# Holding all TensorE instructions in written order through the attention of a two-layer streaming encoder

## The chip, the cores and the metric

The kernel runs on one core of a Trainium2 chip. The metric is device time in microseconds, the median of 3 runs. Five engines work side by side, each through its own instructions in a fixed order: TensorE (PE; its weight loads are PEld), VectorE (DVE), ScalarE (ACT), GpSimd (POOL) and SyncE (SP), which here issues nearly all DMAs. Waits between engines go by semaphores.

## The reference

Input `x` is (1, 2048, 1024) float32. Layer 0 is a gated pooling mixer, layer 1 strictly causal stick-breaking attention with 16 heads of 64 channels; each ends with a gated embedding add. Cut to what matters:

```python
# layer 0
h = rms_norm(x, a_norm);  u, z = split(h @ a_w_in)
pooled = trailing_means(u, windows 2, 4, 8, 16 by channel group) - u
x = x + ((pooled @ w_group) * scale * silu(z)) @ a_w_out
x = x + (p[0] @ ple_w[0]) * sigmoid(x @ ple_gate_w[0])
# shared keys and values, layer 1
k, v = split(rms_norm(x, kv_norm) @ w_kv);  k = rms_norm(heads(k), k_norm)
q, z = split(rms_norm(x, b_norm) @ b_w_in); q = rms_norm(heads(q), b_q_norm)
beta = sigmoid(q . k / 8)
A[t, s] = beta[t, s] * prod over s < j < t of (1 - beta[t, j])     # s < t
x = x + ((A @ v) * silu(z)) @ b_w_out
x = x + (p[1] @ ple_w[1]) * sigmoid(x @ ple_gate_w[1])
```

## The kernel before

**Tiling.** The 2048 frames are four chunks of 512. Activations lie channel-major: 128 channels by 512 frames in a tile. Every matrix product is made of three float32r matmuls per 128 rows of the contraction, high by high, high by low, low by high, where "low part" is what float32r rounding left over (`split`, `put_split`, and L754 for the attention weights).

**Two streams of work.** `stream()` (a generator) yields after each projection matmul: per chunk `first_part` (mixer, output projection, gate, then z, q, k, v of the first eight heads), `second_part` (q, k, v of the other eight), and after all chunks `post` (output projection and gate of layer 1). The projections' weights come in units of 512 KB through nine `wpair` buffers: raw loads (`wraw`) that are split on the spot, or ready pairs that an earlier pass stored (`once`, `wf`). `keep` prepares the 36 units of layer 1's last weights beforehand and stores them; it loads `kraw` and stores `kp`.

The attention is a loop over 160 slots (chunk of queries, head, chunk of keys) of four steps each, 640 steps. One step n does: `turn`, four transposes (L748) of running products into a `psa` bank, copied by ScalarE (L751) with the low part taken by DVE (L754); `front`, two score matmuls (L728, L729) into a `psl` bank, a sigmoid (L731) and, one step later, the running product on DVE (L736, TENSOR_TENSOR_SCAN); and `gather`, two matmuls (L761, L762) into `pso`. The transposes of a slot lag its score products by 5 steps, the gathers by 7 (`LAG_T`, `LAG_G`). In between, `fill` advances the projection stream by a share given by `rate`: about 27 projection matmuls a step in the first chunk, 13 in the second, 7 in the third and fourth. Each of the PSUM tags `psd` (projections), `psl`, `psa` (also for `pst`, small transposes and sums) and `pso` has two banks.

**What sets the order.** The code is written in one order, but the framework schedules: it simulates a timeline by its own costs and issues what it takes to be ready, so instructions of one engine can change places. `tc.keep_in_program_order` ties an instruction behind the one written before it on its engine. Before the change this holds for the running products (L736), the low parts (L754), and one projection matmul in six of `product` when the third or fourth chunk is in the attention (`state["pin"]`, L225).

**Keys and queries** are stored two heads to a tile (`qd`, `kd`: 128 rows, high and low side by side). A key tile is then loaded by two DMAs of 64 partitions, a query pair (`qa` high over low, `qb` low over high) by four.

Of the kernel before, what the change touches and what calls it, by code (L numbers as in the profile page):

```python
# [36 lines left out]
def trunk_kernel(ctx, tc, x, p, a_norm, wu_t, wz_a, w_group, a_scale, a_w_out, kv_norm, w_kv,  # L37
                 k_norm, b_norm, b_w_q, b_w_z, b_q_norm, b_w_out, ple_a, ple_b, gate_a, gate_b, out):
    nc = tc.nc
    V, A, G, T = nc.vector, nc.scalar, nc.gpsimd, nc.tensor  # L40

    cp = ctx.enter_context(tc.tile_pool(name="cp", bufs=1))
    dram = ctx.enter_context(tc.tile_pool(name="dram", bufs=1, space=bass.MemoryType.DRAM))
# [31 lines left out]
    qd = [[scratch(f"qd{s}_{m}", [P, 2, W5]) for m in range(NH // 2)] for s in range(NSUB)]  # L75
    kd = [[scratch(f"kd{s}_{m}", [P, 2, W5]) for m in range(NH // 2)] for s in range(NSUB)]
    vd = [[scratch(f"vd{s}_{b}", [8, P, 4, P]) for b in range(2)] for s in range(NSUB)]
    ve = [[scratch(f"ve{s}_{b}", [4, W5]) for b in range(2)] for s in range(NSUB)]

# [18 lines left out]
    state = {"solo": True, "pin": False, "turn": 0, "lo": 0}  # L98

    def bank(tag, nm):  # L100
        return psum.tile([P, W5], F32, tag=tag, name=nm)
# [117 lines left out]
    def product(ps, us, acts, c0, back):  # L219
        n = len(acts)  # L220
        i = 0
        for u, kts in us:
            for e, kt in enumerate(kts):
                hi, lo = (u[:, l, e, c0 : c0 + P] for l in range(2))
                ins = T.matmul(ps, hi, acts[kt][:, 0], start=(i == 0), stop=False)  # L225
                if state["pin"] and e == 0:
                    tc.keep_in_program_order(ins)
                yield
                T.matmul(ps, hi, acts[kt][:, 1], start=False, stop=False)  # L229
                yield  # L230
# [256 lines left out]
    def kvq(s, kind, b):  # L487
        ck = chunk[s]
        us = take(KT)
        for j in range(4):  # L490
            tk = slice(j * P, (j + 1) * P)
            ps = dense()
            for kt in range(KT):
                u = us[kt][0]
                for xh, wh in ((0, 0), (1, 0), (0, 1)):
                    T.matmul(ps, ck["x2"][kt][:, xh, tk], u[:, wh, 0], start=(kt == 0 and xh == wh),  # L496
                             stop=(kt == KT - 1 and wh == 1))
                    if j == 3 and wh:
                        give_back()
                    yield  # L500
                if j == 0 and kt == 5 and "r2" not in ck:
                    ck["r2"] = token_norm(ck["acc2"], "y")
                if lag and (j, kt) in ((1, 2), (1, 5), (2, 1), (2, 4)):
                    lag.pop(0)()
            rj = ck["r2"][:, j : j + 1]
            settle()
            (valued if kind == "v" else keyed)(s, kind, b, j, ps, rj)
# [25 lines left out]
    def keyed(s, kind, b, j, ps, rj):  # L533
        qs = row("qs")
        q8 = qs.rearrange("q (h d) -> q h d", d=HD)
        A.activation(out=qs, in_=ps, func=AF.Identity, scale=rj)
        sq = tmp("sqq")
        A.activation(out=sq, in_=qs, func=AF.Square)
        ss = pool.tile([P, 8], F32, tag="ssq", name="ssq")
        V.tensor_reduce(out=ss, in_=sq.rearrange("q (h d) -> q h d", d=HD), op=ALU.add, axis=AX.X)  # L540
        rq = pool.tile([P, 8], F32, tag="rq", name="rq")
        rsqrt_mean(rq, ss, HD, "q")
        V.tensor_tensor(out=q8, in0=q8, in1=rq.unsqueeze(2).to_broadcast([P, 8, HD]), op=ALU.mult)
        rows = chunk[s].setdefault((kind, b), [])
        rows.append(qs)
        if j < 3:
            return

        def finish(m):
            pt = turned()  # L550
            for i in range(4):
                T.transpose(pt[:, i, :], rows[i][:, m * P : (m + 1) * P], ident)
            pt = pt.rearrange("q j t -> q (j t)")
            hl = t4("hl")
            if kind == "k":
                split(hl, pt, V)
            else:
                A.activation(out=hl[:, 0], in_=pt, func=AF.Identity, scale=gqk)
                V.scalar_tensor_tensor(out=hl[:, 1], in0=pt, scalar=gqk, in1=f(hl[:, 0]),
                                       op0=ALU.mult, op1=ALU.subtract)  # L560
            nc.sync.dma_start(out=(kd if kind == "k" else qd)[s][4 * b + m], in_=f(hl))

        for m in range(4):
            lag.append(lambda m=m: finish(m))
# [22 lines left out]
    def gate_z(s):  # L587
# [20 lines left out]
        for b in range(1 if first else 0, 4):  # L608
            us = take(4)
            for k in range(2):  # L610
                o = 2 * b + k
                ps = dense()
                for i, _ in enumerate(product(ps, us, ck["x2"], k * P, k)):
                    if first and o == 2 and i == 9:
                        ck["rb2"] = bcast(ck["r2"], "y")
                    if first and o in (2, 3) and i == 21:
                        zr = first[o - 2]
                        V.tensor_tensor(out=zr, in0=zr, in1=ck["rb2"], op=ALU.mult)
                        put(o - 2, zr)
# [72 lines left out]

    def load_q(c, h):
        qa, qb = qryt("qa"), qryt("qb")
        rows = qd[c][h // 2][h % 2 * HD : (h % 2 + 1) * HD]
        for l in range(2):
            nc.sync.dma_start(out=f(qa)[l * HD : (l + 1) * HD], in_=rows[:, l])
            nc.sync.dma_start(out=f(qb)[(1 - l) * HD : (2 - l) * HD], in_=rows[:, l])
        return qa, qb

    def load_k(kc, h):
        kk = keyt("kk")
        rows = kd[kc][h // 2][h % 2 * HD : (h % 2 + 1) * HD]
        for l in range(2):
            nc.sync.dma_start(out=f(kk)[l * HD : (l + 1) * HD], in_=rows[:, l])
        return kk

    def load_v(kc, h):
# [118 lines left out]
        pass  # L827

    until((0, 0))
    state["solo"] = False  # L830
    begin(0)
    begin_v(0)
    for _ in range(24):
        next(run)
    owed = 0.0
    count = 0
# [1 line left out]
    def fill(share):  # L838
        nonlocal owed, count
        owed += share  # L840
        while owed >= 1.0:
            next(run, None)
            owed -= 1.0
            count += 1
            if count % 36 == 0 and kept:
                keep(*kept.pop(0))

    scan = None
    for n in range(4 * len(slots) + LAG_G):
# [3 lines left out]
        low = turn(active[i2], j2) if 0 <= i2 < len(slots) else None  # L853
        due, scan = scan, None
        if i < len(slots):
            state["pin"] = slots[i][0] >= NSUB - 2
            if j == 0 and i + 1 < len(slots):
                begin(i + 1)
            if j == 3 and i + 1 < len(slots):
# [82 lines left out]
```

## Time and profile before

| | us |
|---|---|
| median of 3 runs | 2831.26 (2830.03 to 2836.04) |
| the profiled execution, own time | 2833.48 |
| its span, first to last instruction | 2831.7 |
| busy: PE / DVE / ACT / POOL | 2729.6 / 1832.6 / 1275.0 / 873.3 |
| granted TensorE clock, mean | 0.986 |
| DMA moved | 643 MB, 227 GB/s in the mean |

A span is the time from the first to the last profiled instruction. Busy time is the union of an engine's instructions; PE's are pipelined, so they overlap. "Idle before" counts the time in which an engine did nothing just before an instruction, and the releaser is what ended that wait. Windows are in us from the start of the span. The projections alone run up to about 385 us, when the first score product starts (385.1); the last starts at 2729.3; then the fourth chunk's `post` runs alone.

### The profile page before, as it was taken

The numbers are of one execution on the slowest core, as the hardware profiler recorded it, in microseconds if no ns is written. First come the engines' busy times: TensorE is split into PE (matmuls) and PEld (weight loads), VectorE is DVE, ScalarE is ACT, GpSimd is POOL, SyncE is SP. The second block draws the span as 40 slices with busy tenths as digits, with TensorE's granted clock in tenths as the row PEclk, the third lists the DMA queues.
The fourth block names the chain that finished last, engine by engine and source line by source line (L and its number), as shares of the span: only waits on it lengthen the run. The fifth ranks groups of instructions, "written<-read, shape, count | busy, mean of one in ns | idle before, by whom it ended". The sixth has DMA issues, their size and how long they took to land.

```text
span 2831.7 us, 38727 instructions
## 1 busy us (share of the span) xinstructions
PE 2729.6 (96%) x13400; PEld 2250.0 (79%) x13400; DVE 1832.6 (65%) x2369; ACT 1275.0 (45%) x2496; POOL 873.3 (31%) x699
## 2 busy tenths in 40 slices
PE   7999989989999999999999999989999999999999
PEld 7888867867888888888877887868877888887767
DVE  5645446747344776655568978657667777767772
ACT  4435543445344345444444555444444444444441
POOL 1354533546533244442322434211221101111002
PEclk8999999999999999999999999999999999999999
DMA  5647899979887845668775454676586768666535
GB/s 212 223 142 277 318 340 355 325 218 302 293 289 278 255 142 174 196 226 272 254 242 163 142 158 152 225 262 206 159 276 192 249 207 263 208 194 225 169 121 185
DMA packets 300496, 643.43 MB, mean 227 GB/s; under 512 B 51206, under 2 KB 83974, under 8 KB 300300
## 3 DMA queue, kind: packets, MB, share of 16 engines
q1 hardware_dynamic: 298716, 639.63, 68.6%
q8 instruction: 106, 1.74, 0.2%
q10 hardware_dynamic: 1584, 1.33, 0.2%
q14 instruction: 90, 0.74, 0.1%
HBM read 471.43 MB, written 161.02 MB: 223 GB/s over the span
## 4 chain that ended last, share of the span: by engine, by line
PE 78%; DMA 8%; DVE 7%; ACT 2%; issue 2%; POOL 1%; SPq 1%; ACTq 0%; DVEq 0%; POOLq 0%
PE psd L496 15%; PE psd L225 11%; PE psd L229 11%; PE psd L232 11%; PE psa L748 7%; PE pso L762 4%; PE psl L729 4%; PE psl L728 3%; PE pso L761 3%; DVE pp L736 3%; PE psd L251 2%; PE psd L248 2%; PE psd L246 2%; DMA wpair<-once 2%; DVE at L754 1%
## 5 line engine op out<-in xcount | busy, mean ns | idle before, releaser
L736 DVE TENSOR_TENSOR_SCAN pp<-pp,floor 128x512 f32<-128x512 f32 (+3 forms) x640 | 779.0, 1219 | 5.2 <-ACT pp L731 4.6
L496 PE MATMUL psd<-wpair,x 128*128 128x512 f32 x2304 | 582.9, 395 | 10.0 <-ACT wpair L137 3.9
L754 DVE TENSOR_TENSOR at<-psa,at 128x512 fp32r<-128x512 f32 (+3 forms) x640 | 378.7, 595 | 312.9 <-ACT at L751 311.1
L496 PEld LDWEIGHTS psd<-wpair,x 128*128 128x128 f32 x2304 | 425.4, 189 | 98.6 <-ACT wpair L137 5.8
L751 ACT CAST at<-psa 128x512 fp32r<-128x512 f32 (+3 forms) x640 | 330.9, 523 | 378.3 <-PE psa L748 358.7
L731 ACT ACTIVATE pp<-psl 128x512 f32<-128x512 f32 (+3 forms) x640 | 333.4, 535 | 305.8 <-PE psl L729 194.8
L748 PE MATMUL psa<-ident,pp 128*128 128x128 f32 x2176 | 357.4, 276 | 45.0 <-DVE at L754 23.7
L748 PEld LDWEIGHTS psa<-ident,pp 128*128 128x128 f32 x2176 | 272.9, 141 | 132.0 <-DVE at L754 38.7
L762 PE MATMUL pso<-at,vv 128*128 128x512 f32 (+3 forms) x640 | 275.1, 430 | 0.6 <-DVE at L754 0.6
L728 PE MATMUL psl<-kk,qa 128*128 128x512 f32 (+3 forms) x640 | 244.3, 382 | 13.2 <-DMA kk<-kd 9.8
L761 PE MATMUL pso<-at,vv 128*128 128x512 f32 (+3 forms) x640 | 238.7, 374 | 7.6 <-DMA once<-kp 5.4
L729 PE MATMUL psl<-kk,qb 128*128 128x512 f32 (+3 forms) x640 | 236.0, 370 | 0.0
L225 PE MATMUL psd<-x,wpair 128*128 128x512 f32 x592 | 233.5, 394 | 0.0
L232 PE MATMUL psd<-x,wpair 128*128 128x512 f32 x592 | 232.5, 393 | 0.0
L229 PE MATMUL psd<-x,wpair 128*128 128x512 f32 x592 | 232.5, 393 | 0.0
L225 PE MATMUL psd<-xp,wpair 128*128 128x512 f32 x512 | 203.5, 398 | 0.5 <-DMA wpair<-once 0.5
L229 PE MATMUL psd<-xp,wpair 128*128 128x512 f32 x512 | 201.7, 394 | 0.0
L232 PE MATMUL psd<-xp,wpair 128*128 128x512 f32 x512 | 201.2, 394 | 0.0
L133 POOL TENSOR_TENSOR wpair<-wraw,wpair 128x512 fp32r<-128x512 f32 x98 | 139.0, 1423 | 153.6 <-ACT wpair L131 152.5
L728 PEld LDWEIGHTS psl<-kk,qa 128*128 128x128 f32 x640 | 122.8, 192 | 40.8 <-ACT pp L731 11.2
L465 POOL TENSOR_TENSOR xj<-x 128x512 f32<-128x512 f32 x64 | 106.9, 1675 | 139.6 <-DVE sg L476 131.9
L761 PEld LDWEIGHTS pso<-at,vv 128*128 128x128 f32 x640 | 122.0, 191 | 27.7 <-ACT at L751 11.0
(162 smaller groups left out, 4621.0 us busy)
## 6 DMA issues: line engine op xcount, KB each, us to landing
wpair<-once SPq DMA_DIRECT2D x384, 512.0 KB
once<-wpair SPq DMA_DIRECT2D x80, 512.0 KB
kk<-kd SPq DMA_DIRECT2D x320, 128.0 KB
vv<-vd SPq DMA_DIRECT2D x160, 256.0 KB
wpair<-wf SPq DMA_DIRECT2D x48, 512.0 KB
once<-kp SPq DMA_DIRECT2D x36, 512.0 KB
wraw<-in_a_w_out_dram SPq DMA_DIRECT2D x64, 256.0 KB
wraw<-in_gate_a_dram SPq DMA_DIRECT2D x64, 256.0 KB
```

The costliest lines, as they stand in the source:

```text
L225: ins = T.matmul(ps, hi, acts[kt][:, 0], start=(i == 0), stop=False)
L229: T.matmul(ps, hi, acts[kt][:, 1], start=False, stop=False)
L232: T.matmul(ps, lo, acts[kt][:, 0], start=False, stop=(i == n))
L496: T.matmul(ps, ck["x2"][kt][:, xh, tk], u[:, wh, 0], start=(kt == 0 and xh == wh), stop=(kt == KT - 1 and wh == 1))
L728: T.matmul(ps[:, :w], qa[:, qs], kk[:, :w], start=True, stop=False)
L729: T.matmul(ps[:, :w], qb[:, qs], kk[:, :w], start=False, stop=True)
L731: A.activation(out=pp[:, r0:], in_=ps[:, :w], func=AF.Sigmoid, scale=-1.0)
L736: V.tensor_tensor_scan(out=pp[:, r0:][:, ::-1], data0=pp[:, r0:][:, ::-1], data1=least, initial=1.0 if st["diag"] else st["carry"][j], op0 ...
L748: T.transpose(pt[:, j * P : (j + 1) * P], pp[:, r0 + kt * P : r0 + (kt + 1) * P], ident)
L754: V.tensor_tensor(out=at[:, 1, cs], in0=pt[:, cs], in1=f(at[:, 0, cs]), op=ALU.subtract))
L761: T.matmul(po[:, cs], vv[:, kt, :], at[:, 0, cs], start=(st["diag"] and kt == 0), stop=False)
L762: T.matmul(po[:, cs], vv[:, kt, :], at[:, 1, cs], start=False, stop=(st["last"] and kt == 3))
```

## The change

It does five things.

1. `nc.tensor` is wrapped by a class `T` whose `matmul` and `transpose` call `tc.keep_in_program_order` on every instruction as long as `state["hold"]` is set: from the first attention slot to the last. The partial pin in `product` goes. All of PE's instructions are then recorded at the wrapper's two lines (L46 matmuls, L50 transposes).
2. Three places are moved later in the written order: the sums of squares for `r2` from the sixth to the end of the eight contraction blocks in `kvq`; the broadcast of `r2` in `gate_z` from the 10th to the 21st matmul; and `keep` starts only once chunk 1's first half of heads is done.
3. Before the first step, 60 projection matmuls are written instead of 24.
4. `qd` and `kd` hold one head each, high rows over low rows, so a key tile is one DMA of 128 partitions, a query pair three DMAs instead of four; what was one store is two of 64 partitions.
5. The running products and the low parts were tied already and stay so.

```diff
-    V, A, G, T = nc.vector, nc.scalar, nc.gpsimd, nc.tensor
+    V, A, G = nc.vector, nc.scalar, nc.gpsimd
+    state = {"solo": True, "hold": False, "turn": 0, "lo": 0}
+
+    class T:
+        @staticmethod
+        def matmul(*a, **k):
+            return held_in_order(nc.tensor.matmul(*a, **k))
...
+    def held_in_order(ins):
+        return tc.keep_in_program_order(ins) if state["hold"] else ins
...
-    kd = [[scratch(f"kd{s}_{m}", [P, 2, W5]) for m in range(NH // 2)] for s in range(NSUB)]
+    kd = [[scratch(f"kd{s}_{h}", [2, HD, W5]) for h in range(NH)] for s in range(NSUB)]
...
-                ins = T.matmul(ps, hi, acts[kt][:, 0], start=(i == 0), stop=False)
-                if state["pin"] and e == 0:
-                    tc.keep_in_program_order(ins)
+                T.matmul(ps, hi, acts[kt][:, 0], start=(i == 0), stop=False)
...
-                if j == 0 and kt == 5 and "r2" not in ck:
-                    ck["r2"] = token_norm(ck["acc2"], "y")
                 if lag and (j, kt) in ((1, 2), (1, 5), (2, 1), (2, 4)):
                     lag.pop(0)()
+            if "r2" not in ck:
+                ck["r2"] = token_norm(ck["acc2"], "y")
...
-            nc.sync.dma_start(out=(kd if kind == "k" else qd)[s][4 * b + m], in_=f(hl))
+            for e in range(2):
+                nc.sync.dma_start(out=(kd if kind == "k" else qd)[s][8 * b + 2 * m + e].rearrange("l d n -> d l n"),
+                                  in_=f(hl)[e * HD : (e + 1) * HD])
...
-                    if first and o == 2 and i == 9:
+                    if first and o == 2 and i == 20:
...
-        rows = qd[c][h // 2][h % 2 * HD : (h % 2 + 1) * HD]
+        nc.sync.dma_start(out=f(qa), in_=qd[c][h].rearrange("l d n -> (l d) n"))
         for l in range(2):
-            nc.sync.dma_start(out=f(qa)[l * HD : (l + 1) * HD], in_=rows[:, l])
-            nc.sync.dma_start(out=f(qb)[(1 - l) * HD : (2 - l) * HD], in_=rows[:, l])
+            nc.sync.dma_start(out=f(qb)[(1 - l) * HD : (2 - l) * HD], in_=qd[c][h][l])
...
-        rows = kd[kc][h // 2][h % 2 * HD : (h % 2 + 1) * HD]
-        for l in range(2):
-            nc.sync.dma_start(out=f(kk)[l * HD : (l + 1) * HD], in_=rows[:, l])
+        nc.sync.dma_start(out=f(kk), in_=kd[kc][h].rearrange("l d n -> (l d) n"))
...
-    state["solo"] = False
+    state["solo"], state["hold"] = False, True
     begin(0)
     begin_v(0)
-    for _ in range(24):
+    for _ in range(60):
         next(run)
...
-            if count % 36 == 0 and kept:
+            if count % 36 == 0 and kept and (1, 0) in marks:
                 keep(*kept.pop(0))
...
-            state["pin"] = slots[i][0] >= NSUB - 2
...
-    state["solo"], state["pin"] = True, False
+    state["solo"], state["hold"] = True, False
```

What it does to the order of PE, at step 348 of 640 (third chunk). `psl` rows are score products, `psa` and `pst` transposes, `pso` gathers, `psd` projections. Before:

```order
L728 MATMUL psl<-kk,qa 128x128
L729 MATMUL psl<-kk,qb 128x128
L748 MATMUL psa<-ident,pp 128x128
L762 MATMUL pso<-at,vv 128x256
L728 MATMUL psl<-kk,qa 128x256
L729 MATMUL psl<-kk,qb 128x256
L761 MATMUL pso<-at,vv 128x128
L552 MATMUL pst<-ident,qs 128x128 x4
L748 MATMUL psa<-ident,pp 128x128 x4
L762 MATMUL pso<-at,vv 128x128
```

The same step, with the change:

```order
L50 MATMUL psa<-ident,pp 128x128 x4
L46 MATMUL psl<-kk,qa 128x128
L46 MATMUL psl<-kk,qb 128x128
L46 MATMUL psd<-x_16533,wpair 128x512 x2
L46 MATMUL psd<-x_16654,wpair 128x512 x2
L46 MATMUL pso<-at,vv 128x512 x2
L46 MATMUL psd<-x_16654,wpair 128x512
L46 MATMUL psd<-x_16792,wpair 128x512 x3
```

Before, the pieces of several steps stood together without a projection between them, the two halves of a gather apart; now each step has its four transposes, two scores and two gathers with four and four projections between.

The tail of the attention on PE, step 610 and after. Before:

```order
L748 MATMUL psa<-ident,pp 128x128 x4
L762 MATMUL pso<-at,vv 128x512
L728 MATMUL psl<-kk,qa 128x256
L729 MATMUL psl<-kk,qb 128x256
L728 MATMUL psl<-kk,qa 128x384
L729 MATMUL psl<-kk,qb 128x384
L761 MATMUL pso<-at,vv 128x512
```

And with the change, a few steps earlier:

```order
L46 MATMUL pso<-at,vv 128x128 x2
L46 MATMUL psd<-og,wpair 128x512 x5
L50 MATMUL psa<-ident,pp 128x128 x4
L46 MATMUL psl<-kk,qa 128x512
L46 MATMUL psl<-kk,qb 128x512
L46 MATMUL pso<-at,vv 128x512 x2
```

In both the projection stream has run out some 40 steps before the end, and what follows has no projections between.

SP's queue where the first key tiles are loaded (`kd` keys, `once` and `wraw` weight units, `kraw` the preparation of `keep`). Before:

```order
L678 DMA kraw<-in_b_w_out_dram 128x512
L148 DMA wraw<-in_w_kv_dram 128x512
L705 DMA kk<-kd_0_261 64x512
L152 DMA once_3561<-wpair 128x1024
L705 DMA kk<-kd_0_261 64x512
L561 DMA kd_2_263<-hl 128x1024
```

With the change:

```order
L713 DMA kk<-kd_0_293 128x512
L159 DMA wraw<-in_w_kv_dram 128x512
L163 DMA once_3633<-wpair 128x1024
L713 DMA kk<-kd_1_294 128x512
L159 DMA wraw<-in_w_kv_dram 128x512
```

A key tile is one row instead of two, its store two rows of 64 partitions instead of one of 128, and no `kraw` stands here any more: the first comes some 250 rows later.

More of the change, by code (lines that the diff above doesn't have):

```diff
@@ L39, in trunk_kernel, with transpose @@
     nc = tc.nc
-    V, A, G, T = nc.vector, nc.scalar, nc.gpsimd, nc.tensor
+    V, A, G = nc.vector, nc.scalar, nc.gpsimd
[4 more added lines that the diff above has]
+            return held_in_order(nc.tensor.matmul(*a, **k))
+        @staticmethod
+        def transpose(*a, **k):
+            return held_in_order(nc.tensor.transpose(*a, **k))
+    def held_in_order(ins):
+        return tc.keep_in_program_order(ins) if state["hold"] else ins
     cp = ctx.enter_context(tc.tile_pool(name="cp", bufs=1))
@@ L74, in trunk_kernel @@
     od = [[scratch(f"od{s}_{o}", [P, 2, W5]) for o in range(KT)] for s in range(NSUB)]
-    qd = [[scratch(f"qd{s}_{m}", [P, 2, W5]) for m in range(NH // 2)] for s in range(NSUB)]
-    kd = [[scratch(f"kd{s}_{m}", [P, 2, W5]) for m in range(NH // 2)] for s in range(NSUB)]
+    qd = [[scratch(f"qd{s}_{h}", [2, HD, W5]) for h in range(NH)] for s in range(NSUB)]
+    kd = [[scratch(f"kd{s}_{h}", [2, HD, W5]) for h in range(NH)] for s in range(NSUB)]
     vd = [[scratch(f"vd{s}_{b}", [8, P, 4, P]) for b in range(2)] for s in range(NSUB)]
@@ L96, in trunk_kernel @@
     att = lambda nm: pool.tile([P, 2, W5], F32R, tag="at", name=nm, bufs=3)
-    state = {"solo": True, "pin": False, "turn": 0, "lo": 0}
     def bank(tag, nm):
```

## The prediction, made before the changed kernel was run

> **What bounds the kernel now.** I read the page's engine rows first, then the windows by stage, then who waited for whom.
>
> ```profile
> PE 2729.6 (96%) x13400; PEld 2250.0 (79%) x13400; DVE 1832.6 (65%) x2369; ACT 1275.0 (45%) x2496; POOL 873.3 (31%) x699
> ```
>
> TensorE (PE) is the bound: busy for 2729.6 of 2831.7 us, and the change neither adds nor removes a matmul. What it can win is PE time that is lost between matmuls. The windows say where that lies (span of the window, then busy us of PE, PEld, DVE, ACT, POOL, granted clock, DMA share, GB/s):
>
> ```profile
> 0.00:100.00 100.00, 85.11 (x430) 75.31 (x431) 60.09 (x150) 45.94 (x92) 18.51 (x27) 0.90 0.62 222
> 300.00:700.00 400.00, 369.32 (x1699) 301.71 (x1698) 234.24 (x295) 178.39 (x342) 186.18 (x152) 0.97 0.89 306
> 700.00:1400.00 700.00, 693.85 (x3432) 575.01 (x3431) 409.72 (x533) 312.56 (x625) 278.64 (x226) 1.00 0.73 239
> 1400.00:2200.00 800.00, 766.74 (x3866) 627.69 (x3865) 587.65 (x719) 385.57 (x762) 206.07 (x160) 0.99 0.62 199
> 2200.00:2500.00 300.00, 299.85 (x1539) 249.68 (x1538) 223.15 (x271) 134.27 (x261) 40.85 (x25) 1.00 0.71 229
> 2500.00:2800.00 300.00, 287.81 (x1414) 231.90 (x1413) 204.04 (x245) 126.32 (x246) 40.75 (x28) 0.98 0.58 185
> ```
>
> PE idles 30.7 us in 300:700 (400 - 369.32), 6.2 in 700:1400, 33.3 in 1400:2200, 0.2 in 2200:2500 and 12.2 in 2500:2800. The 14.9 us of the first 100 us lie ahead of the change. So the same work once runs without a gap (2200:2500) and once loses 4% (1400:2200). The waits of PE in 300:700 (first five rows), then in 700:2500 (us in total, times, longest):
>
> ```profile
> PE psa L748 <- DVE pp L736: 8.4, 3, 4.5
> PE pso L761 <- DMA once<-kp: 5.4, 1, 5.4
> PE psl L728 <- DMA kk<-kd: 5.3, 1, 5.3
> PE psd L496 <- ACT wpair L137: 3.9, 4, 1.6
> PE psa L748 <- DVE hl L559: 2.4, 1, 2.4
> ...
> PE psa L748 <- DVE at L754: 15.2, 24, 1.3
> PE psa L748 <- DVE hl L120: 4.6, 2, 3.4
> PE psl L728 <- DMA kk<-kd: 4.2, 1, 4.2
> PE psa L748 <- DVE pp L736: 4.2, 5, 2.3
> PE psd L496 <- DMA wpair<-once: 3.2, 3, 1.5
> ```
>
> Mostly the transposes (L748) wait for VectorE (DVE): for a bank whose low part (L754) is not taken yet, or for a running product (L736). Why there and not elsewhere, two windows tell:
>
> ```profile
> 1895.00:1912.00 17.00, 8.35 (x38) 6.15 (x39) 9.44 (x13) 6.45 (x13) 2.75 (x3) 0.70 1.02 343
> 2000.00:2017.00 17.00, 17.00 (x87) 14.16 (x86) 13.07 (x17) 8.84 (x18) 2.69 (x3) 1.00 0.22 60
> ```
>
> The first is the place of the order rows above: attention steps follow each other with no projection between them, and PE works 8.35 of 17 us. Long stalls are paid twice, since the granted clock halves after them:
>
> ```profile
> 399.80:406.60 6.80, 4.70 (x14) 0.50 1.04 349
> 423.70:427.10 3.40, 3.23 (x11) 0.50 1.04 411
> 573.90:580.70 6.80, 4.27 (x12) 0.50 0.98 295
> 631.90:638.70 6.80, 5.91 (x17) 0.50 0.68 196
> 1440.80:1447.70 6.90, 5.31 (x16) 0.51 1.05 299
> 1898.20:1908.50 10.30, 5.58 (x20) 0.50 1.02 330
> 2126.90:2130.30 3.40, 3.36 (x14) 0.50 0.58 175
> ```
>
> PE's busy time in these is half lost: (4.70 + 3.23 + 4.27 + 5.91)/2 = 9.1 us in 300:700 and (5.31 + 5.58 + 3.36)/2 = 7.1 us in 700:2500.
>
> **What a bunch costs.** A bare step is four transposes, two score products (L728, L729) and two gathers (L761, L762), with nothing of the projections. PE's rows by start, and DVE's two forms with their means in ns:
>
> ```profile
> 2701.50 0.66 PE L748 MATMUL psa<-ident,pp 128*128 128x128 f32 x4
> 2701.91 0.48 PE L762 MATMUL pso<-at,vv 128*128 128x512 f32 x1
> ...
> 2707.39 0.40 PE L728 MATMUL psl<-kk,qa 128*128 128x512 f32 x1
> 2707.63 0.39 PE L729 MATMUL psl<-kk,qb 128*128 128x512 f32 x1
> ```
>
> ```profile
> L736 DVE TENSOR_TENSOR_SCAN pp<-pp,floor 128x512 f32<-128x512 f32 x448 | 620.5, 1386 | 4.9 <-ACT pp L731 4.3
> L754 DVE TENSOR_TENSOR at<-psa,at 128x512 fp32r<-128x512 f32 x448 | 301.3, 676 | 258.1 <-ACT at L751 257.1
> ```
>
> Start to start, four transposes take 0.41 us and a 512-column matmul 0.23, so PE needs 0.41 + 4 x 0.23 = 1.33 us for a bare step; DVE needs 1.39 + 0.68 = 2.06. Bare steps in a row therefore lose 0.73 us each. With seven projection matmuls between, PE needs 1.33 + 7 x 0.23 = 2.94 us and DVE has 0.9 us to spare. Counted over the whole order, 166 of the 640 steps before have no projection matmul up to the next step; in the change it is 34, all among the last 45, where the projections have run out (before: 32 of the last 45). So the change spreads the bunches everywhere but in the tail. The 2.94 us of a step also lengthens the distance that matters: in the last two chunks a transpose comes back to its bank two steps, 5.9 us, later, while in a bunch it comes 2.7 us later, and must find ScalarE's copy and DVE's 0.68 done, often behind a running product's 1.39.
>
> A wait costs a little more than its row shows. The matmul at 2707.39 lasts 0.40 us but the next starts 0.23 later: a gap begins only when the last 0.17 us of the pipe have run out. 44 waits of 700:2500 that I expect to go, times 0.17, are 7.5 us. [...]
>
> **The change part by part**, against the profiled execution (2833.5 us; 2.2 above the median of 2831.3).
>
> *PE order, 700:2500.* Idle 6.2 + 33.3 + 0.2 = 39.7, clock 7.1, hidden 7.5: 54 us. Bounds: all goes (-54), or nothing (0). What stays: the waits for wpair loads, 3.2 us, and 6 us where DVE is fullest, in the third attention chunk, beside the pooling mixer:
>
> ```profile
> 1500.00:1600.00 100.00, 96.19 (x491) 78.95 (x490) 84.10 (x101) 45.09 (x92) 27.78 (x27) 1.00 0.49 151
> ```
>
> At 84% DVE a burst of the mixer can still hold back a transpose. Taken: -45.
>
> *PE order, 300:700, with the head start of 60 instead of 24 and the weight preparation put off.* Idle 30.7, clock 9.1. The three longest waits go: L736 8.4 (a running product has now two steps of 27 projections, 12 us, until its transpose), kp 5.4, kk 5.3; with them the halved clock at 399.8, 573.9 and 631.9, (4.70 + 4.27 + 5.91)/2 = 7.4. Waits for weights, 3.9, and the small ones stay, and I allow 6 us for new ones, since attention can no longer step ahead of a late weight. Taken: -20; bounds -40 and 0 (beyond that, the last rival).
>
> The longest wait of PE in 2100:2140:
>
> ```profile
> PE psa L748 <- DVE hl L120: 1.2, 1, 1.2
> ```
>
> [...] Here the wait for L559, 2.4 us and the only one of its kind, ended at 423.9 us and the clock halved at 423.7, so shorter gaps cost clock too, as at 2126.9 after waits of at most 1.2. [...]
>
> *Tail.* Bare steps 34 against 32, and 79 against 111 projection matmuls in the last 45 steps: 32 x 0.23 = 7 us less PE work to cover DVE there. Bounds 0 and +7; taken +4.
>
> *Keys and queries by head.*
>
> ```profile
> kk<-kd SPq DMA_DIRECT2D x320, 128.0 KB
> once<-kp SPq DMA_DIRECT2D x36, 512.0 KB
> ```
>
> 320 loads become 160 and four query loads three (-64), 64 stores become 128: 160 issues fewer on SP, bytes unchanged. DMA works beside PE (share 0.62 to 0.89), and the kk waits are counted above. 0; uncovered it could cost at most what kk waits cost now (4.2 + 5.3), and gain as much. The prepared weights move 36 x (256 + 512) KB = 28 MB, at 306 GB/s 90 us of DMA, out of 300:700 into 700:1400, where share 0.73 becomes 0.86: hidden, if the loads of wpair stay ahead. The low parts and running products stood in program order before; nothing is added there.
>
> Sum: -45 - 20 + 4 = -61; 2833.5 - 61 = 2772 for the profiled execution, 2770 as median.
>
> **The rivals.**
>
> *DVE is the bound, not the order (15%).* The waits for L754, L736 and L120 only move. For it: 84% DVE in 1500:1600. Against it: 2000:2017 runs 17.00 of 17 us with DVE at 13.07. Then only the DMA waits go: 4.2 + 5.3 + 5.4 and half of 4.70 + 4.27 + 5.58, 7.3: 22 us, 2809.
>
> *All of it goes (12%).* Every wait in 300:2500 disappears as in 2200:2500: 54 + 40 - 4 = 90 us, 2741. For it: the calm window has the same kinds of work. Against it: weights come late in 300:500 whatever the order.
>
> *Late weights stop everything (13%, slower).* In the first kvq of the second half, 24 weight units are loaded raw, split and stored (chain of waits):
>
> ```profile
> 376.19 6.07 DMA wraw<-in_w_kv_dram
> 382.35 0.73 ACT wpair L137
> ```
>
> Such a load takes 6.07 us at worst here, its split 0.73 on ScalarE and as much on DVE. A unit feeds 12 matmuls, 2.8 us, and with its share of attention (12/27 of 1.33) 3.4 us. Loaded one after the other a unit takes 6.07 + 2 x 0.73 = 7.5. Before, attention steps were moved into such holes; now PE stands. 4.1 us x 24 = 98 us: 2868 if all are serial; it turns the sum from 15 of 24 on. Against it: PE idled only 31 us in all of 300:700, so several loads overlap, and the 36 preparations no longer share the queue.
>
> *No change to speak of (5%)*: some of these in balance. That the order is not changed is excluded by its rows.
>
> **How the numbers follow.** Forecast 55%: 2770, by itself 2745 to 2795 (700:2500 between -54 and -30, 300:700 between -33 and -8). Range: down to 2730, which is the second rival with the tail gaining the 7 us that it is feared to lose (2831.3 - 54 - 40 - 7); up to 2832, past the DVE rival, where the gains would be used up; outside remain the late weights and a part of the balance, under 2 in 10. A measurement tells 0.2%, 5.7 us, from no change. Faster: 55 + 15 + 12 less 2 at the edge, 0.80; same 0.07; slower 0.13.
>
> **What would show it.** Right: in the new profile PE is over 98% busy in 1400:2200, the wait of L748 for DVE falls from 19.4 us (15.2 + 4.2) in 700:2500 to under 8, the clock is halved at most four times between 300 and 2500, and the tail's windows look as now. DVE rival: the same waits in the same sum. Late weights: waits for wpair or wraw above 30 us in 300:700. It is wrong as a whole if the waits vanish and the time does not, or if new waits of PE, for kk, vv or wpair, come to more than 20 us after 700.

## The result, and the profile after

| | before | after |
|---|---|---|
| median, us (four runs each) | 2832.19 | 2962.28 (2962.03 to 2962.87) |
| ratio, 95% interval | | 1.0459 (1.0447 to 1.0471) |
| span of the profiled execution, us | 2831.7 | 2960.6 |
| granted TensorE clock, mean | 0.986 | 0.968 |

The change is slower by 130 us. The forecast was 2770, its range 2730 to 2832: wrong in sign, and the time lies far outside. The page's engine row of the changed kernel, and its TensorE clock in 40 slices:

```profile
PE 2761.0 (93%) x13400; PEld 2261.7 (76%) x13400; DVE 1827.4 (62%) x2369; ACT 1275.8 (43%) x2496; POOL 866.3 (29%) x699
PEclk8999989999998999999989999999999999999999
```

The work of the engines is what it was (DVE 1827 against 1833, POOL 866 against 873). TensorE is busy 31 us longer with the same 13400 matmuls: between 300 and 2500 us the clock is halved for 154 us, before for 44. And it stands still 98 us longer. The windows of the changed kernel, with the columns of the prediction's:

```profile
300.00:700.00 400.00, 373.00 (x1689) 302.23 (x1688) 211.47 (x281) 159.84 (x300) 160.28 (x134) 0.95 0.75 245
700.00:1400.00 700.00, 644.45 (x3084) 523.64 (x3082) 386.92 (x494) 300.60 (x603) 281.28 (x230) 0.97 0.76 248
1400.00:2200.00 800.00, 721.67 (x3594) 589.35 (x3593) 533.22 (x659) 360.47 (x710) 203.39 (x163) 0.96 0.59 188
2200.00:2500.00 300.00, 288.61 (x1468) 237.89 (x1467) 213.63 (x258) 129.95 (x257) 39.28 (x27) 0.98 0.66 215
2500.00:2800.00 300.00, 300.00 (x1532) 248.28 (x1531) 224.07 (x267) 132.80 (x262) 43.41 (x26) 1.00 0.66 221
```

In 700:2500 PE idles 145.3 us (1800 - 644.45 - 721.67 - 288.61) where it idled 39.7. Only 2500:2800 is as calm as forecast: 300.00 of 300, clock 1.00. What PE waits for in 700:2500 (us, times, longest):

```profile
PE psa L50 <- DVE pp L744: 62.3, 18, 16.4
PE psa L50 <- DVE at L762: 42.1, 15, 12.9
PE psd L46 <- DMA wpair<-once: 23.4, 24, 8.1
PE psd L46 <- DVE xr L449: 4.0, 1, 4.0
```

The transposes (L50) wait as before for running products and low parts (L744 and L762, formerly L736 and L754), but 104.4 us instead of 19.4, and single waits last up to 16.4 us. No running product takes 16 us: in the rows below it is 1.2. So the next question is what DVE waits for. Its two largest waits over the whole span:

```profile
DVE at L762 <- ACT at L759: 296.5, 248, 6.6
DVE vv L539 <- ACT vv L538: 122.6, 22, 15.6
```

The first was 311.1 before. The second was far smaller before the change, under its old line number:

```profile
DVE vv L530 <- ACT vv L529: 22.5, 12, 4.5
```

L539 (L530 before) takes the low part of a block of *values*. Each of the 32 blocks (128 frames, eight heads) goes this way: the projection's result `vr` is written by ScalarE (L520); SP issues DMAs that copy its rows one frame down into `vs` (L523, L525); GpSimd subtracts (`differences`, L535), ScalarE rounds (L538), DVE takes the low part (L539), SP stores. The timeline of the changed kernel around the longest stall (start, us, engine, and in brackets the idle time before it and what ended it):

```profile
1527.27 0.69 ACT L520 ACTIVATE vr<-psd,r 128x512 f32<-128x512 f32 x1
...
1531.27 0.91 SPq L156 DMA_DIRECT2D wpair<-once  x1
1532.27 1.49 SPq L523 DMA_DIRECT2D vs<-vr  x2
...
1540.82 1.26 POOL L535 TENSOR_TENSOR vs<-vs,vr 128x512 f32<-128x512 f32 x1 [15.07 <-DMA vs<-vr]
1542.11 0.62 ACT L538 CAST vv<-vs 128x512 fp32r<-128x512 f32 x1 [13.18 <-POOL vs L535]
1542.76 0.69 DVE L539 TENSOR_TENSOR vv<-vs,vv 128x512 fp32r<-128x512 f32 x1 [15.04 <-ACT vv L538]
1543.37 1.22 DVE L744 TENSOR_TENSOR_SCAN pp<-pp,floor 128x512 f32<-128x512 f32 x1
1544.73 0.44 PE L50 MATMUL psa<-ident,pp 128*128 128x128 f32 x1 [16.41 <-DVE pp L744]
```

Read upward: the rows are ready at 1528.0, their copy is issued from 4.3 us later on and lands 7 us after its second issue ends; four engines stand in a line behind it. DVE had reached L539 15 us too early, and the running product L744, which needs nothing of the values, waits behind it: the product starts at 1543.4, where L539 ends.

The rows came only a little later than before, by 0.9 to 2.3 us where DVE stood longest. For the last block of four in each half of the third and fourth chunk, in us after the end of L520 (the start of GpSimd's line, the start of DVE's, DVE's idle time):

| half | before: POOL, DVE, idle | after: POOL, DVE, idle |
|---|---|---|
| third chunk, first | 12.9, 17.2, 0.3 | 13.8, 15.7, 15.6 |
| third chunk, second | 11.1, 19.4, 1.6 | 12.9, 14.8, 15.0 |
| fourth chunk, first | 10.5, 24.3, 0.0 | 12.8, 14.8, 14.5 |
| fourth chunk, second | 9.8, 30.3, 0.0 | 10.8, 12.7, 12.9 |

What changed is DVE's own order: the scheduler, which places L539 as it places everything untied, no longer leaves 17 to 30 us of other work between the projection and the line. Over all 32 blocks the line starts 24.0 us after L520 in the mean before, 13.7 with the change. Why it is placed earlier when PE is held cannot be read from a trace.

### The profile page after: what moved, and what is told of

It is laid out like the page before. It is cut to its first block, busy times and chain, and to the rows that moved or that the text cites. A ratio compares the mean times of both kernels' runs of the same rounds, so it can differ in the third digit from the quotient of the medians.

```text
span 2960.6 us, 38154 instructions
## 1 busy us (share of the span) xinstructions
PE 2761.0 (93%) x13400; PEld 2261.7 (76%) x13400; DVE 1827.4 (62%) x2369; ACT 1275.8 (43%) x2496; POOL 866.3 (29%) x699
## 5 line engine op out<-in xcount | busy, mean ns | idle before, releaser
L744 DVE TENSOR_TENSOR_SCAN pp<-pp,floor 128x512 f32<-128x512 f32 (+3 forms) x640 | 775.3, 1211 | 7.4 <-ACT pp L739 6.1
L46 PE MATMUL psd<-wpair,x 128*128 128x512 f32 x2304 | 625.1, 406 | 38.0 <-DMA wpair<-once 21.1
L46 PE MATMUL psd<-x,wpair 128*128 128x512 f32 x2304 | 601.7, 394 | 3.2 <-ACT zr L616 2.0
L762 DVE TENSOR_TENSOR at<-psa,at 128x512 fp32r<-128x512 f32 (+3 forms) x640 | 382.1, 598 | 298.8 <-ACT at L759 296.5
L46 PEld LDWEIGHTS psd<-wpair,x 128*128 128x128 f32 x2304 | 430.1, 193 | 138.9 <-DMA wpair<-once 33.6
L46 PEld LDWEIGHTS psd<-x,wpair 128*128 128x128 f32 x2304 | 428.6, 189 | 93.1 <-ACT sg L481 2.3
L50 PE MATMUL psa<-ident,pp 128*128 128x128 f32 x2176 | 354.1, 276 | 112.6 <-DVE pp L744 65.3
L50 PEld LDWEIGHTS psa<-ident,pp 128*128 128x128 f32 x2176 | 276.2, 141 | 207.3 <-issue 52.5
L46 PE MATMUL psd<-xp,wpair 128*128 128x512 f32 x1536 | 397.2, 400 | 6.6 <-DMA wpair<-once 6.6
L46 PE MATMUL pso<-at,vv 128*128 128x512 f32 (+3 forms) x1280 | 364.2, 366 | 0.2 <-DVE at L762 0.2
L739 ACT ACTIVATE pp<-psl 128x512 f32<-128x512 f32 (+3 forms) x640 | 344.4, 538 | 12.9 <-PE psl L46 9.3
L46 PEld LDWEIGHTS psd<-xp,wpair 128*128 128x128 f32 x1536 | 290.9, 193 | 68.7 <-DMA wpair<-once 8.8
L46 PE MATMUL psl<-kk,qa 128*128 128x512 f32 (+3 forms) x640 | 287.3, 449 | 1.8 <-DMA kk<-kd 1.8
L46 PEld LDWEIGHTS pso<-at,vv 128*128 128x128 f32 x1280 | 243.5, 191 | 55.2 <-DVE at L762 0.5
L46 PE MATMUL psl<-kk,qb 128*128 128x512 f32 (+3 forms) x640 | 236.6, 370 | 0.0
L46 PE MATMUL psd<-og,wpair 128*128 128x512 f32 x744 | 203.1, 395 | 1.6 <-DVE os L775 1.4
L46 PE MATMUL psd<-mp,wpair 128*128 128x512 f32 x768 | 197.1, 398 | 6.8 <-DVE xr L449 6.8
L46 PEld LDWEIGHTS psd<-mp,wpair 128*128 128x128 f32 x768 | 145.1, 192 | 37.7 <-DVE xr L449 7.7
L46 PEld LDWEIGHTS psd<-og,wpair 128*128 128x128 f32 x744 | 138.1, 188 | 31.4 <-DVE os L775 1.7
```

The source lines that it names most:

```text
L46: return held_in_order(nc.tensor.matmul(*a, **k))
L50: return held_in_order(nc.tensor.transpose(*a, **k))
L739: A.activation(out=pp[:, r0:], in_=ps[:, :w], func=AF.Sigmoid, scale=-1.0)
L744: V.tensor_tensor_scan(out=pp[:, r0:][:, ::-1], data0=pp[:, r0:][:, ::-1], data1=least, initial=1.0 if st["diag"] else st["carry"][j], op0 ...
L762: V.tensor_tensor(out=at[:, 1, cs], in0=pt[:, cs], in1=f(at[:, 0, cs]), op=ALU.subtract))
```

## The experiments

The kernel before ran beside each batch, medians 2832.3 to 2833.8; ratios are to it.

**e1: the values' low part on GpSimd.** The order of PE is that of the change, instruction by instruction.

```diff
-        V.tensor_tensor(out=vv[:, :, 1, :], in0=vs, in1=f(vv[:, :, 0, :]), op=ALU.subtract)
+        G.tensor_tensor(out=vv[:, :, 1, :], in0=vs, in1=f(vv[:, :, 0, :]), op=ALU.subtract)
```

> The changed kernel with one instruction type moved: the low part of the values (L539, 32 times) is taken by GpSimd instead of VectorE. PE's order is the same, instruction by instruction. Theory A (blocked queue): L539 stands on VectorE up to 15 us for rows that a DMA shifts by one frame, the running products are tied behind it, and PE, held in written order, stands behind them. Then the waits of PE's transposes for VectorE, 104 us in 700:2300, fall below 40, and the time to 2850 to 2885. Theory B (tight order): the transposes lag their scores too little for any delay on VectorE, L539 is only one of many; then the waits stay above 70 us and the time above 2920.

2890.23 us, ratio 1.0206 (1.0189 to 1.0223): 72 of the 130 us go with one line, 5 us short of what theory A had named. PE's waits in 700:2500:

```profile
PE psd L46 <- DMA wpair<-once: 24.9, 23, 7.5
PE psa L50 <- DVE pp L744: 19.9, 15, 5.7
PE psa L50 <- DVE at L762: 18.3, 12, 3.0
```

The transposes' 104.4 us are 38.2 now; the waits for weights stand.

**e2: the shifted rows issued by ScalarE**, past SP's queue of weight loads.

```diff
-            nc.sync.dma_start(out=vs[lo + 1 : hi + 1], in_=vr[lo:hi])
+            nc.scalar.dma_start(out=vs[lo + 1 : hi + 1], in_=vr[lo:hi])
```

> The changed kernel with the row-shifting DMAs of the values (L523, L525) issued from ScalarE's queue instead of SP's. Theory A says the shifted rows come late because they queue behind up to seven weight loads of 512 KB on SP's queue (1522 to 1532 us): on a queue of their own the wait of GpSimd's L535 for them falls from 251 us to below 120, L539 no longer blocks, time 2855 to 2895. If the rows are late for another reason (the store of ve, or the busy DMA engines), the waits for them stay above 200 us and the time above 2930.

2946.48 us, 1.0402 (1.0383 to 1.042): only 16 us, as the second expectation had it. GpSimd's wait for the rows, in the change and in e2 (idle us, times):

```profile
  DMA vs<-vr: 251.2, 26
```

```profile
  DMA vs<-vr: 230.8, 25
```

GpSimd has little else to do (busy 29% of the span in the change), so this wait overstates the lateness. For the last block of each half, eight in all, the subtraction starts 16.1 us after L520 in the mean of the change and 11.3 us in e2. The way past SP's queue takes off 4.8 us, the smaller part of that; from the end of the last issue to the subtraction it is 6.6 us with SP issuing and 6.3 with ScalarE, so there another issuing engine saves hardly anything. In the longest stall of the change this time is the wait for the rows to land, 7 us beside DMA engines that are busy to 0.81 (last section). DVE's wait ahead of L539 falls from 122.6 to 96.2 us.

**e3: the change without the hold**, all else kept.

```diff
-    state["solo"], state["hold"] = False, True
+    state["solo"], state["hold"] = False, False
```

> The changed kernel with the hold off: PE is scheduled freely, all else (storage by head, late weight preparation, 60 matmuls ahead, later sums and broadcast) stays. If the hold alone costs the 130 us (theories A and B), the time is 2810 to 2850, about that of the kernel before. If the other parts cost a share (late weight preparation in the second chunk, or stores of 64 partitions), it is above 2870.

2826.32 us, 0.9979 (0.9968 to 0.9991). The hold costs 136 us, and the rest of the change, with the old partial pin gone too, gains 7. DVE idles ahead of L539 here as well, but PE hardly waits for the running products (first row over the whole span, second in 300:2800):

```profile
DVE vv L539 <- ACT vv L538: 52.8, 13, 15.0
PE psa L50 <- DVE pp L744: 9.1, 8, 1.8
```

In a free order PE has other work there: 9.1 us of waits against 62.3 in the change, in the same 300:2800.

**e4: keys and queries stored by head, alone**, in the kernel before (the lines of `qd`, `kd`, `load_q`, `load_k` and the store).

> The kernel before with keys and queries stored by head, nothing else. All theories: 2822 to 2842, no change that can be measured or a few us less, since the loads lie beside PE's work; above 2860 would say that the stores of 64 partitions are to blame.

2844.35 us, 1.004 (1.0026 to 1.0054): 11 us slower, not nothing, and 2 us above the range expected.

So 57 us were left to explain: e1 at 2890 against 2833. Two theories: in a held order the parts of a step stand too close (last score product of a slot to its first transposes: 4.6 to 5.0 us of PE work in the last two chunks, where the scheduler's order had a median of about 11 and 9), or late weights stop everything. All of e5 to e8 keep e1's line on GpSimd.

**e5: one step more between scores and transposes.**

```diff
-LAG_T, LAG_G = 5, 7
+LAG_T, LAG_G = 6, 8
...
-            if j == 3 and i + 1 < len(slots):
-                begin_v(i + 1)
+            if j == 0 and i:
+                begin_v(i)
```

> The change with the low part of the values on GpSimd (as e1, 2890 us) and in addition the transposes six steps instead of five behind their scores and the gathers eight instead of seven; the loads of values are issued one step later so that they do not wait on SP for the buffer. The order stays held on TensorE. In the program's order the matmul work between the last score product of a slot and its first transpose grows from 4.6 to 5.0 us to 7.3 us in the last two chunks. Theory A (what is left of the loss after e1 is lack of distance: a held order gives the scan and the copies no slack): the waits of the transposes for VectorE fall from 38 us in 700:2300 to under 12, the time to 2835 to 2855. Rival B (late weights stop everything): the waits for wpair stay, time 2880 to 2895. Rival C (the longer distance holds running products and values longer, and ScalarE or the loads wait for buffers): 2895 to 2930.

2859.5 us, 1.0094 (1.0077 to 1.0111): 31 us less, half of the rest. Between the two expectations: A was right in direction, but of the transposes' waits 20 us stay in 700:2500, not under 12. PE's waits in 300:2800 say what is left:

```profile
PE psd L46 <- DMA wpair<-once: 27.0, 23, 4.0
PE psa L50 <- DVE at L762: 23.0, 30, 2.5
PE psd L46 <- ACT wpair L148: 17.5, 8, 7.2
```

**e6: only the projections held; e7: only the attention held.** In e6 the five calls of `turn`, `front` and `gather` go past the wrapper; in e7 they alone are tied.

```diff
-            T.transpose(pt[:, j * P : (j + 1) * P], pp[:, r0 + kt * P : r0 + (kt + 1) * P], ident)
+            nc.tensor.transpose(pt[:, j * P : (j + 1) * P], pp[:, r0 + kt * P : r0 + (kt + 1) * P], ident)
```

> As e1, but only the projections, norms' products and other matmuls outside attention keep program order; scores, transposes and gathers may be moved by the scheduler as before. Theory A (lack of distance between an attention step's parts): the scheduler moves transposes back to a median of 8.6 us behind the scores, the time falls to 2830 to 2855. Rival B (late weights): the projections still stand in program order and a late weight still holds what stands behind it, 2870 to 2895.

> As e1, but only scores, transposes and gathers keep their order among themselves; the scheduler may move the projections around them. Theory A (lack of distance): the distance from the last score product to the first transpose falls to a median of 4.8 to 5.3 us with a lowest decile of 1.8 us, so the waits of the transposes for VectorE grow above e1's 38 us in 700:2300 and the time to 2890 to 2940. Rival B (late weights): the projections can be put off when a weight is late, the waits for wpair fall under 10 us, 2840 to 2870.

e6: 2804.98 us, 0.99 (0.9882 to 0.9917), the first that clearly beats the kernel before, and below both ranges expected. e7: 2841.32, 1.0034 (1.0021 to 1.0047). In e6, 1400:2200 is what the prediction wanted of the change, and its waits in 300:2800 are short:

```profile
1400.00:2200.00 800.00, 793.24 (x4061) 656.25 (x4060) 602.42 (x737) 402.77 (x787) 230.21 (x174) 1.00 0.66 214
```

```profile
PE psd L46 <- DMA wpair<-once: 17.0, 8, 6.0
PE psd L46 <- ACT wpair L148: 14.2, 7, 5.9
PE psa L756 <- DVE at L762: 11.0, 19, 1.6
PE psa L756 <- DVE pp L744: 7.3, 5, 2.6
```

e7 speaks against A in its simple form: its transposes stand as close behind their scores as in e1 (medians 4.8 and 5.3 us), and they wait 25.9 us, not more than e1's 45.2 in the same 300:2800. It is not the distance alone: the same distance costs less when the projections may move around the waits. e7's time lies in the range of rival B, but B's mark, waits for weights under 10 us, was not reached: they are 21.4 (42.4 in e1). e6 waits 31.4 us for weights, and is the faster of the two.

**e8: e3 with the low part on GpSimd.**

> e3 (the change without the hold, 2826 us) with the low part of the values on GpSimd. If VectorE's wait for the values also costs time in a free order, up to 9 us are to be had (VectorE idles 8.9 us in gaps over 3 us ahead of that line in the kernel before): 2815 to 2824. If the scheduler's distance covers it, or GpSimd's own line gets longer by as much, no difference: 2824 to 2832.

2837.25 us, 1.0016 (1.0002 to 1.003), 11 us above e3 and outside both ranges expected. No gain: in a free order the line on DVE cost nothing that moving it would save. So e6's gain comes from holding the projections: 32 us against e8, whose 1400:2200 reads

```profile
1400.00:2200.00 800.00, 774.09 (x3884) 637.14 (x3883) 573.63 (x698) 377.43 (x748) 225.06 (x172) 0.99 0.62 206
```

**e9: e6 with the low part back on DVE; e10: e6 with e5's distance; e11: e6, held only once the second chunk's first half is through**, about 880 us.

```diff
+        state["hold"] = (1, 0) in marks
         if i < len(slots):
```

> e6 (projections held in order, attention free to move, 2805 us) with the low part of the values back on VectorE, as the change has it. So it is the change with attention alone set free. Theory A (values that come late stop VectorE whatever the order of TensorE; under the full hold this cost 72 us): 2840 to 2875. Theory D (a stop of VectorE costs only where the transposes stand close behind their scores; with a median of 8.6 to 9 us instead of 4.8 most of it is absorbed, as in the free order, where 2826 and 2837 us show no gain from GpSimd): 2795 to 2815.

> e6 with the longer distance of e5 (transposes six steps behind their scores, gathers eight). In the program's order the median from the last score product of a slot to its first transpose grows from 8.6 to 9.5 us. If distance is what still costs in e6 (18 us of waits of transposes for VectorE are left), 2785 to 2800; if it is used up and buffers are now the limit, 2800 to 2825.

> e6, but the projections are held in order only once the first half of the second chunk's projections is through (about 880 us); before that everything may be moved. Late weights (e6 waits 17.0 us for stored and 14.2 us for split weights, of this about 20 us before 880): if the free order plans around them, the waits for weights before 880 us fall to under 8 us and the time to 2785 to 2797; if the weights are late whatever the order, 2797 to 2810.

e9: 2858.19, 1.0084 (1.0069 to 1.0099); with the projections held the line on DVE costs 53 us even where attention may move, and theory D is refuted. DVE's wait there:

```profile
DVE vv L539 <- ACT vv L538: 86.1, 19, 15.2
```

Holding the projections is also enough to bring the line forward: it starts 14.3 us after L520 in the mean (13.7 in the change, 25.5 in e3, 24.0 before). e10: 2812.3, 0.9928 (0.9913 to 0.9943), 7 us above e6; no more is to be had from distance. e11: 2800.71, **0.9888 (0.9872 to 0.9905)**, the best of all, though its gain on e6 is within the intervals. The waits for raw and stored weights in 300:2800 fell from 31.4 to 19.3 us, but those before 880 us only to 14.9, not under the 8 that the faster expectation needed.

**e12: the differences one block later**, the line on DVE, all held.

```diff
-            settle()
+            settle(1)
```

> The change as it is, full hold and the low part of the values on VectorE, but the differences of a block of values are issued one block later (24 projection matmuls, 8 to 11 us with attention between). Theory A (VectorE stands behind values whose rows land late): VectorE's idle time ahead of that line falls from 106 us to under 40 and the time to 2885 to 2915, as with GpSimd in e1 (2890). Rival (it was the load on VectorE, not the wait, that e1 took away): 2945 to 2965.

2958.08, 1.0441 (1.0425 to 1.0456): 4 us, within the intervals, and the number is the rival's. But the edit missed its aim: DVE's wait ahead of the line fell only from 122.6 to 107.2 us. The last block of four is settled right after the loop, as before, and there DVE still stood:

```profile
1535.95 0.69 DVE L539 TENSOR_TENSOR vv<-vs,vv 128x512 fp32r<-128x512 f32 x1 [17.08 <-ACT vv L538]
```

**e13: the line and its store 36 projection matmuls later in every block; e14: the same with attention free.**

```diff
-        V.tensor_tensor(out=vv[:, :, 1, :], in0=vs, in1=f(vv[:, :, 0, :]), op=ALU.subtract)
-        nc.sync.dma_start(out=vd[s][b][:, :, j, :]...
+        pend.append([36, lambda: low_part(s, b, j, vs, vv)])
```

> The change as it is, full hold, the low part of the values on VectorE; only this instruction and the store behind it are issued 36 projection matmuls later (12 to 16 us with attention between), in every block, the last of four included, which e12 left where it was: in e12 VectorE still idled 15 to 17 us ahead of the last block's line. Theory A (VectorE stands behind the last block's rows, which land 11 to 14 us after the projection): VectorE's idle time ahead of that line falls from 106 us to under 30, the waits of the transposes for VectorE in 700:2300 from 104 to under 45, the time to 2880 to 2910, as with GpSimd in e1 (2890). Rival (VectorE's load by this line): 2940 to 2965.

> e9 (projections held, attention free, the low part on VectorE, 2858 us) with the same deferral by 36 projection matmuls. Theory A (the 53 us between e9 and e6 are VectorE's wait for late rows as well): 2800 to 2820, as e6 (2805). Rival (GpSimd relieves VectorE): 2840 to 2860.

e13: 2913.28, 1.0289 (1.0272 to 1.0307). DVE's wait ahead of the line (L544 in this kernel):

```profile
DVE vv L544 <- ACT vv L538: 61.8, 17, 14.0
```

Half of the wait went (122.6 to 61.8) and with it 49 us, with the instruction still on DVE. e14: 2827.36, 0.9977 (0.9964 to 0.999), 31 of the 53 us of e9, with 49.9 us of wait left of 86.1. Both fall short of A's number, e13 by 3 us and e14 by 7, and of the waits A named: the deferral was too short for some blocks (the longest wait is still 14.0). Both lie clear of the rival's range: what was won was won by less waiting, with the load where it was.

**The account.** 130 us = 72 (values that come late stop DVE, and held PE with it: e1; 49 of them go in e13 with the line still on DVE) + 31 (what one step more of distance takes back: e5) + 27. In the last 27 (profiled executions) PE is busy 17.5 us longer (2747.1 in e5 against 2729.6 before) and idle 9.9 us longer (112.0 against 102.1). So the larger share is matmuls at the lower clock: it is halved for about 99 us of 300:2500 in e5 against 44 before. Of the waits behind it, those for weights are the nearest candidate: in 300:2800 they are 7.6 us before, 44.4 after, 44.5 in e5, while the transposes' waits in e5, 27.4, are below the 44.5 before. But e6 stands 31.4 us for weights and is faster than before, and no run takes these waits away alone, so this part is measured and its cause is not shown.

## Why the prediction was wrong

**PE order, 700:2500, taken -45, bounds -54 and 0: the step that failed.** It counted what a held order takes away, the bunches, and gave "nothing" as the worst it can do; the idle time there rose by 105.6 us. Two things were left out. The change part by part ends with "The low parts and running products stood in program order before; nothing is added there". For these two lines that is true, but in a free order PE had other work while DVE stood (e3); held, it passes such stops on. And the hold moved a third line of DVE, the values', to where it waits (22.5 us before, 122.6 after). And the only distance weighed was that of a bank's return (two steps, 5.9 us), not that between scores and transposes, which the scheduler had at 9 to 11 us and the written order has at 5.

**What a bunch costs, 0.73 us a bare step: right for runs of them, wrong as a count.** The prediction counted 166 bare steps before and 34 after. (A bare step in these counts has no matmul besides its own; of projections alone, 174 steps before have none.) By the same rule e3 has 252 and is 0.2% faster than before, e6 has 162 and is 1% faster. Counted in runs (first 595 steps; bare steps, and those of them in runs of three or more) it fits: before 134 and 47, e3 211 and 48, e8 236 and 50, e7 194 and 44, but e6 125 and 4, e11 133 and 7; and PE's busy time in 1400:2200 is 767, 781 and 774 us before, in e3 and in e8, and 793 and 795 in e6 and e11. A single bare step seems to cost nothing, perhaps since the next step's projections make it good. That is a reading of the orders beside the times, not an experiment on one run.

**The gain itself was there.** Holding the projections after the first half of chunk two, with attention free and the values' line off DVE, is 36 us better than the same kernel with all free (e11 against e8). That is of the size of the -45. The forecast gave it to a change that also held the attention, which costs 85 us (e1 against e6).

**PE order, 300:700, taken -20: came out at about 0.** The named waits went as said (kk 1.8 us left, kp and L736 none), and others took their place. PE's waits there:

```profile
PE psd L46 <- ACT wpair L148: 16.6, 7, 5.5
PE psd L46 <- DMA wpair<-once: 4.3, 1, 4.3
PE psd L46 <- DVE xr L449: 2.8, 1, 2.8
PE psl L46 <- DMA kk<-kd: 1.8, 1, 1.8
```

PE idles 27.0 us instead of 30.7, with the clock at 0.95 instead of 0.97. 6 us were allowed for new waits; weights alone brought 17 (20.9, where 3.9 were kept).

**Tail, taken +4: about 0, the lower of its bounds.** From the running product of step 592 to the end it is 197 us before and 190 after. That is no gain: 465 projection matmuls start behind it instead of 492, and the other 27, 27 x 0.23 = 6 us, stand ahead of it now.

**By head, taken 0 with an end of +9.5 if uncovered: +11 by itself** (e4). Which wait it goes through is not settled; in e3, beside the other edits, it does not show.

**The rivals.** "Late weights stop everything" had the right sign and was priced at up to 98 us; its mark, more than 30 us of waits for weights in 300:700, was not reached (20.9). It explains at most the last 27 us, and mostly after 700, where the prediction did not look for it. "DVE is the bound" had the right engine for the wrong reason: DVE is busy 62%, and it is what DVE waits for that counts. No rival named the values. L530's 22.5 us stood in the same view of DVE's waits that the prediction could have read: the question "what does DVE wait for, and what is tied behind it" was not asked.

**What would show it.** 98% in 1400:2200 was 90%, under 8 us of transposes waiting was 104.4, at most four halvings between 300 and 2500 were 20 (7 before). The mark for wrong as a whole, new waits for kk, vv or wpair over 20 us after 700, was just about reached (23.4 for wpair in 700:2500, where 3.7 stood before), but it was not the main loss.

## What to carry to other kernels

Before an engine is tied to its written order, list for every engine that it waits on what that engine itself may stand behind, above all instructions that wait for a DMA and are not part of the tied work: in a free order such stops cost little here (9.1 us of PE's waits for running products in e3), and a tie passes each of them on (62.3 us in the change), and can move them too. Tie one stream (here the projections, whose hold was worth 36 us) and leave the other free to move; where both must be tied, the written distances have to cover the worst landing time seen, not the mean (36 projection matmuls in e13 still left DVE 61.8 us of waiting, the longest 14.0). And a count of bunched steps says little until it is taken by the length of the runs.

## What the runs showed of the hardware

In the changed kernel a wait of 2.0 us cost nearly as much clock as one of 16.4, and one of 3.0 us none. Around the stall of 1528.3 to 1544.7, and around a wait of 2.0 us that ended at 1244.9 (windows with the columns as above; the granted clock is the number before the DMA share):

```profile
1528.30:1531.60 3.30, 0.02 (x1) 0.00 (x0) 0.00 (x0) 0.63 (x2) 0.00 (x0) 1.00 1.04 389
1531.60:1544.70 13.10, 0.00 (x0) 0.00 (x0) 1.94 (x3) 0.62 (x1) 1.26 (x1) 0.50 0.64 212
1544.70:1548.60 3.90, 3.87 (x10) 3.13 (x11) 3.44 (x4) 1.18 (x2) 0.00 (x0) 0.50 0.40 113
1534.00:1541.00 7.00, 0.00 (x0) 0.00 (x0) 0.00 (x0) 0.00 (x0) 0.18 (x1) 0.50 0.81 269
...
1243.00:1244.90 1.90, 0.01 (x1) 0.01 (x1) 0.00 (x0) 1.17 (x3) 0.54 (x2) 0.99 0.96 375
1244.90:1248.30 3.40, 3.40 (x9) 2.83 (x10) 1.56 (x2) 1.87 (x5) 2.01 (x3) 0.50 1.01 401
1248.30:1252.00 3.70, 3.70 (x19) 3.06 (x19) 1.82 (x2) 1.71 (x3) 1.29 (x1) 1.00 1.03 407
```

During the long stall the clock drops 3.3 us after PE stops and is back 3.9 us after it starts: 10 matmuls in 3.9 us at 0.50, about 2 us lost (an estimate: half of the time). After the short wait, which eight matmuls of one column each precede, it is half for 3.4 us, 9 matmuls where the next 3.7 us hold 19, 1.7 us lost by the same estimate. A wait of 2.0 us that ended at 1347.4 was followed by 3.4 us at 0.50 too. But a wait of 3.0 us that ended at 2178.0 cost no clock:

```profile
2175.00:2178.00 3.00, 0.03 (x1) 0.01 (x1) 2.46 (x4) 1.28 (x4) 1.97 (x2) 1.00 0.22 76
2178.00:2185.00 7.00, 6.45 (x34) 5.25 (x35) 5.32 (x7) 3.52 (x7) 1.65 (x2) 1.00 0.76 245
```

By the clock record of this trace, the 20 halved stretches that begin in 300:2500 last 3.4 us (nine of them), 6.8 (three), 10.2 (three), 13.7 (four) and 17.1 (one), and their starts lie whole multiples of 3.41 us apart (1347.3, 1531.6 and 2026.5, for instance: 54 and 145 times). Why the wait of 3.0 us cost no clock is not shown; no run moves one of these waits.

In the first view, the fourth row is the wait for the shifted rows: hardly an engine computes, and 254 KB need 7 us while the DMA engines are busy to 0.81 and move about 1.9 MB (7 us at 269 GB/s), so mostly what was issued ahead. With the copies issued from ScalarE (e2) this time is hardly shorter, 6.3 against 6.6 us in the mean of eight blocks.
